# Aligned SBUF places, one sum of squares for two query tiles, and a moved filler in a two-layer trunk kernel

## The chip, the cores and the metric

The kernel runs on one core of one Trainium2 chip. The metric is the device time of one execution in microseconds (us), the median over several executions.

## The reference

A two-layer trunk step for 512 sample tokens and 128 prompt tokens, width 2048, in float32. Each layer is a pre-RMSNorm with an adaptive scale and shift (adaLN, computed from a condition vector by a 2048-row matrix), one input projection, mixers, one output projection, and a gated residual:

```python
m = jax.nn.silu(cond) @ w + b            # adaLN: shift, scale, gate
h = rms_norm(x, g) * (1 + scale) + shift
p = split_cols(h @ w_in, SPLIT)
y = concat(mixers(p)) * silu(gates)
x = x + gate * (y @ w_out)
```

The even layer mixes with banded grouped-query attention (8 heads over 2 key heads) and a gated width-3 convolution. The odd layer mixes with differential attention (two softmax maps per head, 4 heads) and with dense grouped-query attention (8 heads). Each query head of 128 columns is divided by its root mean square over the columns before it meets the keys; that is the sum of squares this change touches.

## The kernel before

The 640 tokens stand as columns, in two halves of 320 (`HV`). Every activation and every weight is held as a high and a low part, so each projection tile of 128 output columns is made of three matmuls per 128 input rows: high by high (L364), high by low (L365), low by high (L366). In later stages pairs of output tiles are made by a seven-product scheme (`run_pairs`, L667 to L669, products M1 to M7). ScalarE (ACT) rounds a weight tile to its high part (L328), VectorE (DVE) subtracts to get the low part (L329); both run a few tiles ahead of TensorE (PE), and SyncE (SP) fetches raw weights further ahead (L341). A list scheduler fixes each engine's order before the run.

The stages are: a start that loads x and computes part of adaLN on PE; the even input projection with the banded attention of four pairs of query tiles woven between its tiles (`jobs`, L1435); the rest of that projection in pairs; the even output projection; the odd input projection's gates, keys and values; the odd queries with attention (eight tiles for dense heads and eight for differential heads, in four pairs each); and the last output projection, whose tiles n = 2 to 5 are made singly (`project`, L1306) and n = 6 to 15 as five pairs p = 0 to 4.

**Query norms.** Each query tile arrives in two PSUM banks. `q_gen` (L784; `q_rider` L806 for the second dense head) copies it, squares it (ACT, L789), and calls `q_sums` (L830): three matmuls of 256 columns against a 128x32 matrix of ones (L833), at three places of the PE array, and an ACT copy of 96x256 (L836). `q_places` (L839) makes two 96x96 transposes of that copy (L842), ACT gathers six columns (L845), and GpSimd (POOL) raises 128x6 values to the power -0.5 (L851). That happens for all 24 query tiles, `q0` and `q1` of 12 pairs. The softmax of a head (`soft`, L879) takes the norms as a scale: ACT L883 and L888 use `rq`.

**The filler.** `fill2` computes one adaLN block (layer 1, block 11) on DVE beside the last output projection. It is a generator: for each of 16 row tiles POOL fetches 256 KB (L218) into one of two places, and DVE does two multiply-adds of 128x512 (`adaS<-adaw` or `adaS<-tables`, L213), then PE folds the result (L252, L259). The second place becomes a slice of `tables` at product M1 of p = 0 (`fin_rests`). Each single tile from n = 4 takes one step per quarter of its weights, so the last single tile, n = 5, which runs its token halves one after the other, takes eight. The products M6, M2, M3 and M4 of each pair take steps as well, and `begin` (L1375) drains what is left at p = 3. The block's result `hgt` is needed for output tiles 12 to 15.

**Places.** SBUF tiles are allocated in pools, one behind the other in each partition; before the change most streaming tiles start at byte 160 within a 256-byte line, while `raw`, `wh`, `wl`, `h` and `xb` start at byte 0.

The order of the weights' quarters at n = 5 is fixed in `project`:

```python
for hv in ([HV] if n < n0 - 1 else [HV[1:], HV[:1]]):
    for qd in range(4):
        proj_q(pp, parts[t + qd], qd, qd, hv)
        run_ahead(min(t + qd + 1, len(quarters) - 3))
        advance(attn, 1 if len(hv) == 2 else 2)
        if n >= fill_at:
            next(fill, None)
```

Of the kernel before, what the change touches and what calls it, by code (L numbers as in the profile page):

```python
# [20 lines left out]
P = 128  # L21
# [33 lines left out]
def trunk_kernel(ctx: ExitStack, tc: tile.TileContext, I: dict, O: dict):  # L55
# [47 lines left out]
    ident = const.tile([P, P], F32, name="ident")  # L103
    half = const.tile([P, 8], F32, name="half")
    V.memset(half[:, 0:7], -0.5)
    peps = half[:, 7:8]
    V.memset(peps, P * EPS)
# [656 lines left out]
    def k_gen(ap, pp, tag, src, gain, new_out):  # L764

        raw = ctx_keys(ap, src)
        x = stage(ap, pp)
        yield
        ss = small.tile([P, 5], F32, tag="ss", name="ss")
        kg = ap.tile([P, 5, P], F32, tag="rp", name="kg", bufs=3)  # L770
        junk = ap.tile([P, P], BF16, tag="junk", name="junk", bufs=1)
# [12 lines left out]
    def q_gen(ap, pp, tag, gain, then=None):  # L784
        x = ap.tile([P, NT], F32, tag="stg", name="qx", bufs=2)
        sq = ap.tile([P, NT], F32, tag="stg", name="qsq", bufs=2)
        for i, sl in HV:
            A.activation(x[:, sl], pp[i][:, 0:HALF], AF.Copy, scale=gain)
            A.activation(sq[:, sl], pp[i][:, 0:HALF], AF.Square)  # L789
        sw = ap.tile([P, NS], F32, tag="rp", name="qsw", bufs=st["rp"])  # L790
        for d in range(4):
            nc.sync.dma_start(sw[32 * d:32 * d + 32, :], x[32 * (d ^ 1):32 * (d ^ 1) + 32, 0:NS])
        yield
        m = ap.tile([P, NS], F32, tag="rp", name="qm", bufs=st["rp"])
        V.tensor_mul(m, x[:, 0:NS], cosT)
        sb = q_sums(ap, sq)
        yield
        V.tensor_mul(sw, sw, sinT)
        V.tensor_add(m, m, sw)
        hi, lo = q_places(ap, tag, sb)  # L800
        split(hi[:, 0:NS], lo[:, 0:NS], m)
        split(hi[:, SPLIT], lo[:, SPLIT], x[:, SPLIT])
        if then:
            attn.append(then())

    def q_rider(j, tag, gain, then=None):  # L806
        ap, (g, turned) = pools["cur"], gain
# [11 lines left out]
        sb = q_sums(ap, sq)  # L819
        yield  # L820
        V.tensor_add(m, m, sw)
        hi, lo = q_places(ap, tag, sb)
        split(hi[:, 0:NS], lo[:, 0:NS], m)
        A.activation(hi[:, SPLIT], x[:, SPLIT], AF.Copy, scale=g)
        V.scalar_tensor_tensor(out=lo[:, SPLIT], in0=x[:, SPLIT], scalar=g, in1=hi[:, SPLIT],
                               op0=ALU.mult, op1=ALU.subtract)
        if then:
            attn.append(then())

    def q_sums(ap, sq):  # L830
        ss = psT()
        for g, o in enumerate((0, 256, 384)):
            PE.matmul(ss[32 * g:32 * g + 32, 0:256], ones, sq[:, o:o + 256], start=True, stop=True,  # L833
                      tile_position=(0, 32 * g))
# [4 lines left out]
    def q_places(ap, tag, sb):  # L839
        t = psT()  # L840
        for j in range(2):
            PE.transpose(t[:, j * 96:(j + 1) * 96], sb[:, j * P:(j + 1) * P], ident[0:96, 0:96])  # L842

        u = small.tile([P, 6], F32, tag="ss", name="u")
        A.activation(u.rearrange("p (j g) -> p j g", j=2),  # L845
                     t[:, 0:192].rearrange("p (j g x) -> p j g x", j=2, g=3)[:, :, :, 0], AF.Identity, bias=peps)

        while len(attn) >= st["sets"]:
            advance(attn, 1)
        r6 = small.tile([P, 6], F32, tag="r" + tag, name="r" + tag, bufs=2)  # L850
        G.tensor_tensor(r6, u, half[:, 0:6], op=ALU.pow)  # L851
        r = [r6[:, c:c + 1] for c in (0, 3, 1, 4, 5)]
# [169 lines left out]
    nsink = const.tile([P, 8], F32, name="nsink")  # L1022
    nlam = const.tile([P, 1], F32, name="nlam")

# [5 lines left out]
    ydram = [dram.tile([P, NT], F32, name=f"yd{k}") for k in range(KT)]  # L1030
    x0dram = [dram.tile([P, 4 * NT + 1], F32, name=f"x0d{g}") for g in range(4)]
    kdram = [dram.tile([P, NT], F32, name=f"kd{k}") for k in range(10)]
# [24 lines left out]

    xTm = [sp.tile([P, 4 * NT + 1], F32, name=f"xT{g}") for g in range(4)]
    xT = [t[:, 0:4 * NT].rearrange("p (j t) -> p j t", j=4) for t in xTm]
# [61 lines left out]
    def keep(ui, n, pp):  # L1121
        g = {(6, 0): 0, (6, 4): 1, (7, 0): 2, (7, 4): 3}.get((ui, n))
        if g is not None:
            V.tensor_copy(xTm[g][:, 4 * NT:], pp[1][:, 0:1])
            nc.gpsimd.dma_start(x0dram[g], xTm[g])

# [10 lines left out]

    def q_job(tag, gain, then=None):
        return lambda pp: q_gen(pools["cur"], pp, tag, gains[gain], then)

# [67 lines left out]
    def c_job(i):  # L1208
        def f(pp):
            ap = pools["cur"]  # L1210
            z = ap.tile([P, 644], F32, tag="z", name="z", bufs=1)
            for c in (0, 513, 514, 643):
# [4 lines left out]
            V.tensor_mul(z[:, 515:643], pp[1][:, NS - HALF:HALF], u[:, SPLIT])  # L1217
            t = ap.tile([P, 642], F32, tag="rp", name="cv", bufs=3)
            V.tensor_scalar(t, z[:, 0:642], conv_w[:, 0, i:i + 1], None, ALU.mult)
# [86 lines left out]
    def project(w, cols, n0, maker, job, begin, done, tail, n_lead=3, flip=0, fill=None, rests=lambda p, name: 0.0,  # L1306
# [16 lines left out]
        for n in range(n_lead, n0):  # L1323
# [323 lines left out]
    def odd_start():  # L1647
# [5 lines left out]
        V.tensor_mul(lp, lam4[:, 0:4:2, :], lam4[:, 1:4:2, :])  # L1653
        ls = small.tile([P, 2], F32, tag="ls", name="ls", bufs=1)
        V.tensor_reduce(ls, lp, axis=AX.X, op=ALU.add)
# [14 lines left out]
    def diff_gen(ap, h, v, kq):  # L1670
# [34 lines left out]
        def weigh(u):  # L1705
# [10 lines left out]
            A.activation(on, o, AF.Copy, scale=rls[u])  # L1716
            ssq = small.tile([P, 1], F32, tag="ssq", name="ssq")
# [3 lines left out]
            rn = rns[u] = small.tile([P, 1], F32, tag="rn", name="rn")  # L1721
            G.tensor_tensor(rn, ssq, half[:, 0:1], op=ALU.pow)
            ons[u] = on
# [261 lines left out]
    def with_rest(tag, gain, rest, *a):  # L1985
        def f(pp):
            g = q_gen(pools["cur"], pp, tag, gains[gain])
# [9 lines left out]
    for h in range(4):  # L1997
        jobs.append((OD["cq"] + h * P, q_job("q0", "c_q_norm")))
        jobs.append((OD["cq"] + (4 + h) * P, with_rest("q1", "c_q_norm", head_rest, h, done0 + 4 + h)))
# [132 lines left out]
```

## Time and profile before

| what | value |
|---|---|
| median of 3 runs | 2235.76 us (2233.33 to 2236.55) |
| the profiled execution | 2232.07 us |
| its span, first to last instruction | 2230.1 us |
| busy: PE, DVE, ACT, POOL | 2198.8, 1740.5, 1139.5, 264.4 us |
| mean granted TensorE clock | 0.997 |

The profiled execution lies 3.69 us below the median of the runs, and its own time is 1.97 us longer than its span. In the rows of a timeline the first number is the start in us from the span's start and the second the duration; matmuls overlap, so the pace of PE is read from the distance between starts, not from durations. A bracket at a row's end gives the time the engine stood idle before it, and what it waited for.

### The profile page before, as it was taken

The page shows a single profiled execution, that of the slowest core. Times are in us where ns is not written, and L with a number is a line of the kernel's source. Part 1 is how long each engine was busy: PE and PEld are TensorE (multiplying, and loading weights), DVE is VectorE, ACT ScalarE, POOL GpSimd, SP SyncE. Part 2 cuts the span into 40 slices and gives each one's busy share as a digit, 9 for nine tenths or more (in the row PEclk, how much of TensorE's full clock was granted, in tenths as well). Part 3 has the DMA queues.
Part 4 walks back from the last instruction along what each step waited for, and adds up shares of the span by engine and source line. Part 5 has one row for each costly group of instructions (what it writes and reads, how often), then busy time and mean ns, then how long its engine had stood idle before and what let it go on. Part 6 is the DMA issues. An engine that isn't in the chain of part 4 may idle for free. (4 is left out here: it accounts for less than half of the span.)

```text
span 2230.1 us, 41120 instructions
## 1 busy us (share of the span) xinstructions
PE 2198.8 (99%) x15516; PEld 2126.8 (95%) x15516; DVE 1740.5 (78%) x3031; ACT 1139.5 (51%) x2445; POOL 264.4 (12%) x421
## 2 busy tenths in 40 slices
PE   7999999999999999999999999999999999999999
PEld 5899999999999999999999999999999999999999
DVE  5659898989788977877788878978667566677875
ACT  4335453535334445444654466554578766663343
POOL 3221001000000100000111112211010011111110
PEclk9999999999999999999999999999999999999999
DMA  9985556565453435844675434545532233347641
GB/s 354 342 291 180 163 167 212 175 197 167 149 160 119 145 102 171 261 127 132 218 250 155 149 92 123 177 137 160 173 98 81 73 105 110 119 139 255 200 131 52
DMA packets 380375, 368.47 MB, mean 165 GB/s; under 512 B 18946, under 2 KB 326624, under 8 KB 379664
## 3 DMA queue, kind: packets, MB, share of 16 engines
q1 hardware_dynamic: 357248, 284.78, 41.9%
q0 software_dynamic: 22064, 78.83, 10.1%
q8 instruction: 122, 2.00, 0.4%
q10 hardware_dynamic: 864, 2.23, 0.3%
q14 instruction: 77, 0.63, 0.1%
HBM read 312.41 MB, written 48.11 MB: 162 GB/s over the span
## 5 line engine op out<-in xcount | busy, mean ns | idle before, releaser
L328 ACT ACTIVATE wh<-raw 128x512 fp32r<-128x512 f32 (+1 forms) x352 | 210.6, 600 | 320.5 <-PE pb L365 206.7
L667 PE MATMUL pq<-h,wh 128*128 128x320 f32 x1152 | 359.2, 312 | 0.0
L669 PE MATMUL pq<-h,wl 128*128 128x320 f32 x1152 | 356.4, 309 | 2.7 <-DVE wl L329 2.7
L668 PE MATMUL pq<-h,wh 128*128 128x320 f32 x1152 | 356.5, 309 | 0.0
L364 PE MATMUL pa<-h,wh 128*128 128x320 f32 x944 | 300.8, 319 | 0.0
L365 PE MATMUL pa<-h,wh 128*128 128x320 f32 x944 | 295.4, 313 | 2.0 <-DVE h L329 1.9
L364 PE MATMUL pb<-h,wh 128*128 128x320 f32 x944 | 295.4, 314 | 0.0
L366 PE MATMUL pa<-h,wl 128*128 128x320 f32 x944 | 293.8, 311 | 0.0
L366 PE MATMUL pb<-h,wl 128*128 128x320 f32 x944 | 293.5, 311 | 0.1
L329 DVE TENSOR_TENSOR wl<-raw,wh 128x512 fp32r<-128x512 f32 (+1 forms) x352 | 228.5, 650 | 82.3 <-ACT wh L328 75.5
L365 PE MATMUL pb<-h,wh 128*128 128x320 f32 x944 | 292.4, 310 | 0.0
L667 PE MATMUL pq<-T,wh 128*128 128x320 f32 x864 | 268.6, 311 | 0.0
L669 PE MATMUL pq<-T,wl 128*128 128x320 f32 x864 | 267.1, 309 | 0.4 <-DVE wl L329 0.4
L668 PE MATMUL pq<-T,wh 128*128 128x320 f32 x864 | 266.9, 309 | 0.0
L328 ACT ACTIVATE wh<-sx 128x512 fp32r<-128x512 f32 x216 | 135.7, 631 | 181.3 <-PE pq L668 110.2
L669 PEld LDWEIGHTS pq<-h,wl 128*128 128x128 f32 x1152 | 216.7, 188 | 3.0 <-DVE wl L329 3.0
L667 PEld LDWEIGHTS pq<-h,wh 128*128 128x128 f32 x1152 | 216.8, 188 | 1.6 <-issue 1.6
L668 PEld LDWEIGHTS pq<-h,wh 128*128 128x128 f32 x1152 | 216.9, 188 | 0.4 <-issue 0.4
L282 DVE SCALAR_TENSOR_TENSOR acc<-adaw,sT,acc 128x1024 f32<-128x1024 f32 x150 | 189.5, 1277 | 0.0
L364 PEld LDWEIGHTS pa<-h,wh 128*128 128x128 f32 x944 | 177.9, 189 | 11.3 <-issue 10.2
L365 PEld LDWEIGHTS pa<-h,wh 128*128 128x128 f32 x944 | 178.3, 189 | 7.1 <-issue 4.5
L329 DVE TENSOR_TENSOR wl<-sx,wh 128x512 fp32r<-128x512 f32 x216 | 147.7, 688 | 43.6 <-ACT wh L328 40.7
(426 smaller groups left out, 4984.0 us busy)
## 6 DMA issues: line engine op xcount, KB each, us to landing
adaw<-in_ada_w SPq DMA_DIRECT2D x80, 512.0 KB, 4.0
raw<-in_ev_w_in SPq DMA_DIRECT2D x130, 256.0 KB, 3.3
raw<-in_od_w_in SPq DMA_DIRECT2D x112, 256.0 KB, 3.1
w<-in_od_w_in SPq DMA_DIRECT2D x48, 512.0 KB, 4.4
ada<-in_ada_w SPq DMA_DIRECT2D x11, 2048.0 KB, 13.8
adaw<-in_ada_w POOLq DMA_DIRECT2D x70, 256.0 KB, 3.4
w<-in_ev_w_in SPq DMA_DIRECT2D x27, 512.0 KB, 3.8
adah<-in_ada_w SPq DMA_DIRECT2D x20, 512.0 KB, 9.1
```

The costliest lines, as they stand in the source:

```text
L282: V.scalar_tensor_tensor(out=acc[c], in0=w, scalar=sT[:, kt, c:c + 1], in1=acc[c], op0=ALU.mult, op1=ALU.add)
L328: A.activation(hi, x, AF.Copy)
L329: V.tensor_sub(lo, x, hi)
L364: PE.matmul(ps, wh[:, i, :], hi[:, sl], start=(j == js[0] if alone else (pos == 0 and j == 0)), stop=False)
L365: PE.matmul(ps, wh[:, i, :], lo[:, sl], start=False, stop=False)
L366: PE.matmul(ps, wl[:, i, :], hi[:, sl], start=False, stop=(j == js[1] - 1 if alone else (pos == 3 and j == 3)))
L667: PE.matmul(ps, wh[:, j, :], hi, start=(first and h == 0 and j == 0), stop=False, skip_group_check=True)
L668: PE.matmul(ps, wh[:, j, :], lo, start=False, stop=False, skip_group_check=True)
L669: PE.matmul(ps, wl[:, j, :], hi, start=False, stop=(final and h == 1 and j == 3), skip_group_check=True)
```

## The change

Four edits, one diff.

1. **Places.** Small tiles are merged or padded so that the streaming tiles start at multiples of 256 bytes: `half` gets 13 columns, `nlam` moves into a spare column of `vec`, `xTm`, its DRAM copy, `junk`, `z` and `cv` are padded, `ls` and `rn` share other tiles. Work is unchanged by this, except that the copy out of `xTm` names its columns.
2. **Sums.** The squares of `q0` are kept (in a tag that has room) until `q1` comes; then one `q_sums` does four matmuls of 384 columns, one ACT copy of 128x384, three 128x128 transposes, one gather of 12 columns and one power of 128x12, and fills in both tiles' norms.
3. **Order of the jobs.** In the even stage `b2` stands before `q6`, `q7` instead of behind them.
4. **The filler.** Beside the last single tile the filler steps only with the first half of the tokens that it makes, four steps fewer; from p = 1 on, product M5 takes half a step twice.

```diff
-    half = const.tile([P, 8], F32, name="half")
-    V.memset(half[:, 0:7], -0.5)
-    peps = half[:, 7:8]
+    half = const.tile([P, 13], F32, name="half")
+    V.memset(half[:, 0:12], -0.5)
+    peps = half[:, 12:13]
...
-    def q_gen(ap, pp, tag, gain, then=None):
+    def q_gen(ap, pp, tag, gain, then=None, keep=("rp", 3)):
         x = ap.tile([P, NT], F32, tag="stg", name="qx", bufs=2)
-        sq = ap.tile([P, NT], F32, tag="stg", name="qsq", bufs=2)
+        if tag == "q0":
+            sq = st["sq0"] = ap.tile([P, NT], F32, tag=keep[0], name="qsq", bufs=keep[1])
+        else:
+            sq = ap.tile([P, NT], F32, tag="stg", name="qsq", bufs=2)
...
-        sb = q_sums(ap, sq)
+        if tag == "q1":
+            sb = q_sums(ap, st["sq0"], sq)
...
-        hi, lo = q_places(ap, tag, sb)
+        r = q_norms(sb) if tag == "q1" else []
+        hi, lo = q_places(ap, tag, r)
...
-    def q_sums(ap, sq):
+    def q_sums(ap, *sqs):
         ss = psT()
-        for g, o in enumerate((0, 256, 384)):
-            PE.matmul(ss[32 * g:32 * g + 32, 0:256], ones, sq[:, o:o + 256], start=True, stop=True,
-                      tile_position=(0, 32 * g))
-        sb = ap.tile([96, 256], F32, tag="qs", name="qs", bufs=1)
-        A.copy(sb, ss[0:96, 0:256])
+        for g in range(4):
+            PE.matmul(ss[32 * g:32 * g + 32, 0:384], ones, sqs[g // 2][:, g % 2 * 256:g % 2 * 256 + 384],
+                      start=True, stop=True, tile_position=(0, 32 * g))
+        sb = ap.tile([P, 384], F32, tag="qs", name="qs", bufs=1)
+        A.copy(sb, ss[:, 0:384])
         return sb
...
+    def q_norms(sb):
+        while len(attn) >= st["sets"]:
+            advance(attn, 1)
+        t = psT()
+        for j in range(3):
+            PE.transpose(t[:, j * P:(j + 1) * P], sb[:, j * P:(j + 1) * P], ident)
+        r = small.tile([P, 12], F32, tag="rq", name="rq", bufs=2)
+        A.activation(r.rearrange("p (j g) -> p j g", j=3),
+                     t[:, 0:384].rearrange("p (j g x) -> p j g x", j=3, g=4)[:, :, :, 0], AF.Identity, bias=peps)
+        G.tensor_tensor(r, r, half[:, 0:12], op=ALU.pow)
+        both = [[r[:, c + 2 * i:c + 2 * i + 1] for c in (0, 4, 8, 5, 9)] for i in range(2)]
+        st["q0"][2].extend(both[0])
+        return both[1]
...
-                    if n >= fill_at:
+                    if n >= fill_at and (len(hv) == 2 or hv[0][0]):
                         next(fill, None)
...
-    jobs = [u0, k0, v0, g0, q0, q1, g1, c0, b0, h0, q2, q3, u1, c1, b1, k1, v1, q4, q5, h1, u2, c2, q6, q7, b2, h2, g2, g3]
+    jobs = [u0, k0, v0, g0, q0, q1, g1, c0, b0, h0, q2, q3, u1, c1, b1, k1, v1, q4, q5, h1, u2, c2, b2, q6, q7, h2, g2, g3]
...
-        return float(name in ("M6", "M2", "M3", "M4"))
+        return {"M5": 0.5 if p else 0.0, "M6": 1.0, "M2": 1.0, "M3": 1.0, "M4": 1.0}.get(name, 0.0)
```

How the order moves is shown at two places. The first is PE at the first query pair of the even stage. Before, the sums of `q0` stand between two steps of the projection, and their transposes seven matmuls further on (`h_…` is the activation, `wh` and `wl` the weight's parts, `pa` and `pb` the banks):

```order
L366 MATMUL pa<-h_719,wl 128x320
L833 MATMUL T<-qsq,ones 32x256 x3
L364 MATMUL pa<-h_726,wh 128x320
L365 MATMUL pa<-h_726,wh 128x320
L366 MATMUL pa<-h_726,wl 128x320
L364 MATMUL pb<-h_516,wh 128x320
L365 MATMUL pb<-h_516,wh 128x320
L366 MATMUL pb<-h_516,wl 128x320
L364 MATMUL pb<-h_523,wh 128x320
L842 MATMUL T<-ident,qs 128x96 x2
```

After the change that place holds projection matmuls only, and the one insert for the pair stands where the second tile's sums stood:

```order
L365 MATMUL pb<-h_725,wh 128x320
L366 MATMUL pb<-h_725,wl 128x320
L838 MATMUL T<-qsq,ones 32x384 x4
L364 MATMUL pa<-h_907,wh 128x320
L365 MATMUL pa<-h_907,wh 128x320
L366 MATMUL pa<-h_907,wl 128x320
```

Two inserts per pair became one, of four wider matmuls.

The second place is DVE beside the last single tile of the last output projection, from the low part of that tile's third quarter to the first of the pairs' rows. Before, four filler rows (`adaS<-adaw`) stand ahead of `xr<-pa`, the row that finishes the preceding half tile:

```order
L329 TENSOR_TENSOR wl<-raw,wh 128x512
L213 SCALAR_TENSOR_TENSOR adaS<-adaw,sT,adaS 128x512
L329 TENSOR_TENSOR T_24797<-sx,T_24797 128x960
L329 TENSOR_TENSOR wl<-raw,wh 128x512
L213 SCALAR_TENSOR_TENSOR adaS<-adaw,sT,adaS 128x512
L329 TENSOR_TENSOR wl<-raw,wh 128x512
L606 TENSOR_TENSOR sx<-w_25244,raw 128x512
L213 SCALAR_TENSOR_TENSOR adaS<-adaw,sT,adaS 128x512 x2
L606 TENSOR_TENSOR sx<-w_25244,raw 128x512
L329 TENSOR_TENSOR wl<-raw,wh 128x512
L1291 SCALAR_TENSOR_TENSOR xr<-pa,hgt_137,xr 128x320
```

After the change they are gone from there, and one low part (`wl<-raw`) has moved behind the first sum `sx`:

```order
L329 TENSOR_TENSOR wl<-raw,wh 128x512
L329 TENSOR_TENSOR T_24632<-sx,T_24632 128x960
L329 TENSOR_TENSOR wl<-raw,wh 128x512
L606 TENSOR_TENSOR sx<-w_25071,raw 128x512
L329 TENSOR_TENSOR wl<-raw,wh 128x512
L606 TENSOR_TENSOR sx<-w_25071,raw 128x512
L329 TENSOR_TENSOR wl<-raw,wh 128x512
L1299 SCALAR_TENSOR_TENSOR xr<-pa,hgt_137,xr 128x320
```

Some rows further on, behind the difference `sf` of the first pair, filler rows and low parts stand in the same order in both kernels (the change has it with the same rows, its lines eight higher; the filler is two row tiles further back):

```order
L611 TENSOR_TENSOR sf<-w_25242,w_25244 128x1024
L213 SCALAR_TENSOR_TENSOR adaS<-tables,sT,adaS 128x512 x2
L213 SCALAR_TENSOR_TENSOR adaS<-adaw,sT,adaS 128x512
L1291 SCALAR_TENSOR_TENSOR xr<-pb,hgt_137,xr 128x192
L1291 SCALAR_TENSOR_TENSOR xr<-pb,hgt_137,xr 128x128
L213 SCALAR_TENSOR_TENSOR adaS<-adaw,sT,adaS 128x512
L329 TENSOR_TENSOR wl<-w_25242,wh 128x512
L213 SCALAR_TENSOR_TENSOR adaS<-tables,sT,adaS 128x512 x2
L329 TENSOR_TENSOR wl<-w_25242,wh 128x512
```

So a low part of the first pair's first product still stands behind two filler rows that read a second fetch into `tables`.

The fold of that block also moves. PE's rows L252 and L259 stood 20 matmuls apart inside p = 3; after the change L252 is issued at the end of p = 3's product M1, and L259 stands five matmuls behind it.

More of the change, by code (lines that the diff above doesn't have):

```diff
@@ L770, in k_gen @@
         kg = ap.tile([P, 5, P], F32, tag="rp", name="kg", bufs=3)
-        junk = ap.tile([P, P], BF16, tag="junk", name="junk", bufs=1)
+        junk = ap.tile([P, 160], BF16, tag="junk", name="junk", bufs=1)[:, 0:P]
         r = key_rows(x, ss, kg, junk, gain)
@@ L828, in q_rider, with q_places @@
             attn.append(then())
-    def q_sums(ap, sq):
+    def q_sums(ap, *sqs):
         ss = psT()
-        for g, o in enumerate((0, 256, 384)):
-            PE.matmul(ss[32 * g:32 * g + 32, 0:256], ones, sq[:, o:o + 256], start=True, stop=True,
-                      tile_position=(0, 32 * g))
-        sb = ap.tile([96, 256], F32, tag="qs", name="qs", bufs=1)
-        A.copy(sb, ss[0:96, 0:256])
-        return sb
[L839 to L846, printed above, removed]
+        for g in range(4):
[3 more added lines that the diff above has]
+        A.copy(sb, ss[:, 0:384])
+        return sb
+    def q_norms(sb):
         while len(attn) >= st["sets"]:
             advance(attn, 1)
-        r6 = small.tile([P, 6], F32, tag="r" + tag, name="r" + tag, bufs=2)
-        G.tensor_tensor(r6, u, half[:, 0:6], op=ALU.pow)
-        r = [r6[:, c:c + 1] for c in (0, 3, 1, 4, 5)]
+        t = psT()
[8 more added lines that the diff above has]
+        return both[1]
+    def q_places(ap, tag, r):
+        while len(attn) >= st["sets"]:
+            advance(attn, 1)
         hi, lo = (ap.tile([P, NT], F32R, tag=tag + t, name=tag + t, bufs=st["sets"]) for t in "hl")
@@ L1022, in trunk_kernel @@
     nsink = const.tile([P, 8], F32, name="nsink")
-    nlam = const.tile([P, 1], F32, name="nlam")
+    nlam = vec[:, 159:160]
     fill0 = ada_wide([(0, 8), (1, 4), (1, 0), (1, 6), (0, 10)])
@@ L1030, in trunk_kernel @@
     ydram = [dram.tile([P, NT], F32, name=f"yd{k}") for k in range(KT)]
-    x0dram = [dram.tile([P, 4 * NT + 1], F32, name=f"x0d{g}") for g in range(4)]
+    x0dram = [dram.tile([P, 4 * NT + 16], F32, name=f"x0d{g}") for g in range(4)]
     kdram = [dram.tile([P, NT], F32, name=f"kd{k}") for k in range(10)]
@@ L1054, in y_maker @@
         return make
-    xTm = [sp.tile([P, 4 * NT + 1], F32, name=f"xT{g}") for g in range(4)]
+    xTm = [sp.tile([P, 4 * NT + 64], F32, name=f"xT{g}") for g in range(4)]
     xT = [t[:, 0:4 * NT].rearrange("p (j t) -> p j t", j=4) for t in xTm]
@@ L1136, in v_job, with q_job @@
         return lambda pp: v_gen(pools["cur"], pp, src, new_out, *a)
-    def q_job(tag, gain, then=None):
-        return lambda pp: q_gen(pools["cur"], pp, tag, gains[gain], then)
+    def q_job(tag, gain, then=None, **kw):
+        return lambda pp: q_gen(pools["cur"], pp, tag, gains[gain], then, **kw)
     def y_pair(i):
@@ L1210, in f @@
             ap = pools["cur"]
-            z = ap.tile([P, 644], F32, tag="z", name="z", bufs=1)
+            z = ap.tile([P, 656], F32, tag="z", name="z", bufs=1)
             for c in (0, 513, 514, 643):
@@ L1217, in f @@
             V.tensor_mul(z[:, 515:643], pp[1][:, NS - HALF:HALF], u[:, SPLIT])
-            t = ap.tile([P, 642], F32, tag="rp", name="cv", bufs=3)
+            t = ap.tile([P, 656], F32, tag="rp", name="cv", bufs=3)[:, 0:642]
             V.tensor_scalar(t, z[:, 0:642], conv_w[:, 0, i:i + 1], None, ALU.mult)
@@ L1653, in odd_start @@
         V.tensor_mul(lp, lam4[:, 0:4:2, :], lam4[:, 1:4:2, :])
-        ls = small.tile([P, 2], F32, tag="ls", name="ls", bufs=1)
+        ls = small.tile([P, 2], F32, tag="s4", name="ls")
         V.tensor_reduce(ls, lp, axis=AX.X, op=ALU.add)
@@ L1716, in weigh @@
             A.activation(on, o, AF.Copy, scale=rls[u])
-            ssq = small.tile([P, 1], F32, tag="ssq", name="ssq")
+            both = small.tile([P, 2], F32, tag="ssq", name="ssq")
+            ssq, rns[u] = both[:, 0:1], both[:, 1:2]
             junk = ap.tile([P, 256], BF16, tag="junk", name="junk")
@@ L1720, in weigh @@
             G.tensor_scalar(ssq, ssq, 1.0 / 256, EPS, ALU.mult, ALU.add)
-            rn = rns[u] = small.tile([P, 1], F32, tag="rn", name="rn")
-            G.tensor_tensor(rn, ssq, half[:, 0:1], op=ALU.pow)
+            G.tensor_tensor(rns[u], ssq, half[:, 0:1], op=ALU.pow)
             ons[u] = on
@@ L1986, in f @@
         def f(pp):
-            g = q_gen(pools["cur"], pp, tag, gains[gain])
+            g = q_gen(pools["cur"], pp, tag, gains[gain], keep=("kk", 2))
             next(g)
@@ L1997, in trunk_kernel @@
     for h in range(4):
-        jobs.append((OD["cq"] + h * P, q_job("q0", "c_q_norm")))
+        jobs.append((OD["cq"] + h * P, q_job("q0", "c_q_norm", keep=("x2", 1))))
         jobs.append((OD["cq"] + (4 + h) * P, with_rest("q1", "c_q_norm", head_rest, h, done0 + 4 + h)))
```

8 lines of the change are left out of this document (4 added, 4 removed).

## The prediction

> **What bounds the kernel now.** I read the page's head first, then the waits of PE, then the stretches of the timeline that the change touches.
>
> ```profile
> PE 2198.8 (99%) x15516; PEld 2126.8 (95%) x15516; DVE 1740.5 (78%) x3031; ACT 1139.5 (51%) x2445; POOL 264.4 (12%) x421
> ```
>
> PE is busy for all but 1% of the span, so time is saved in two ways only: by taking instructions from PE, or by ending an idle stretch of PE. The waits of PE (line waited for, total, times, longest) show how little the second can give:
>
> ```profile
> PE T L1070 <- DMA xb<-in_x_sample: 6.6, 2, 5.0
> PE pq L669 <- DVE wl L329: 3.1, 2, 2.7
> PE T L195 <- DMA ada<-in_ada_w: 2.4, 2, 1.7
> PE T L697 <- DVE m L743: 2.0, 1, 2.0
> ```
>
> The first row is the start, where x lands. The 2.7 us of the second row lie behind the last projection's single tile, where the filler is changed.
>
> **The sums, edit 2: the main term.** PE around the insert of the first pair's second tile, its transposes for the first tile, and the filler's fold, which sends four groups where the sums send three:
>
> ```profile
> 193.51 0.31 PE L364 MATMUL pb<-h,wh 128*128 128x320 f32 x1
> 193.66 0.33 PE L842 MATMUL T<-ident,qs 96*128 96x96 f32 x2
> ...
> 194.15 0.31 PE L364 MATMUL pb<-h,wh 128*128 128x320 f32 x1
> ...
> 194.88 0.31 PE L366 MATMUL pb<-h,wl 128*128 128x320 f32 x1
> 195.12 0.63 PE L833 MATMUL T<-qsq,ones 128*32 128x256 f32 x6
> 195.68 0.42 PE L364 MATMUL pa<-h,wh 128*128 128x320 f32 x1
> 195.94 0.31 PE L365 MATMUL pa<-h,wh 128*128 128x320 f32 x1
> ```
>
> ```profile
> 484.40 0.31 PE L366 MATMUL pb<-h,wl 128*128 128x320 f32 x1
> 484.64 0.64 PE L252 MATMUL T<-acc,ones 128*32 128x256 f32 x8
> ...
> 485.46 0.30 PE L365 MATMUL pa<-h,wh 128*128 128x320 f32 x1
> ```
>
> ```profile
> 32.32 1.93 PE L195 MATMUL T<-ada,sT 128*32 128x256 f32 x32 [1.75 <-DMA ada<-in_ada_w]
> 35.16 0.64 PE L195 MATMUL T<-adah,sT 128*32 128x256 f32 x8
> ```
>
> A projection matmul follows the last after 0.147 us (194.15 to 194.88 is five of them). From the matmul ahead of the insert to the second behind it, 194.88 to 195.94, are 1.06 us; two steps of 0.147 would fill 0.29, so three groups cost 0.77 us. The fold's four groups take 484.40 to 485.46, the same 1.06: groups at different places of the array run beside each other, and a fourth is free. What more columns cost comes from the third fence: 32 records take 1.93 us and 8 take 0.64, so 24 more take 1.29, and four at a time, which is one pass of 256 columns, 0.215. Each matmul has two records (144 records for 72 matmuls), so two passes; 128 columns more are half a pass each, 0.215 in all. An insert after the change is 0.77 + 0.215 = 0.985 us, and 24 x 0.77 = 18.5 us become 12 x 0.985 = 11.8: **6.7 us less**.
>
> The bounds: if 384 columns cost no more than 256, 12 x 0.77 = 9.2 and the gain is 9.3; if the groups ran behind each other, the 0.56 us body (195.12 to 195.68) would grow by 4/3 x 384/256 to 1.12 and the insert to 1.33, 16.0 in all and a gain of 2.5. The fold's row is nearest, so I keep 6.7.
>
> Transposes: 193.51 to 194.15 are 0.64 us for three projection matmuls, which alone take 0.44, so two 96-wide ones cost 0.20. For more of them:
>
> ```profile
> 1485.17 0.31 PE L669 MATMUL pq<-T,wl 128*128 128x320 f32 x1
> 1485.32 0.71 PE L697 MATMUL T<-ident,sq 128*128 128x128 f32 x5
> ...
> 1486.01 0.31 PE L668 MATMUL pq<-T,wh 128*128 128x320 f32 x1
> ```
>
> Five cost 0.84 less 0.29, 0.55; each further one is (0.55 - 0.20) / 3 = 0.12, three cost 0.32. 24 x 0.20 = 4.8 become 12 x 0.32 = 3.8: 1.0 us less. Some inserts stand directly beside other small matmuls and share the fixed part, so of 7.7 I count **7.5 us**. All of it lies on PE, with no wait behind it.
>
> **What the later norms cost.** Norms of both tiles now come from one power of 128x12. The tightest pair is the first dense one:
>
> ```profile
> 1619.74 1.68 POOL L851 TENSOR_TENSOR rq<-u,half 128x6 f32<-128x6 f32 x1 [2.74 <-ACT u L845]
> ```
>
> ```profile
> 1623.08 0.29 ACT L883 ACTIVATE nm<-nm,rq 128x1 f32<-128x1 f32 x1 [1.24 <-DVE nm L881]
> ...
> 1624.80 0.93 ACT L983 ACTIVATE p<-p,rl 128x768 f32<-128x768 f32 x1
> ```
>
> ```profile
> 1626.58 0.38 PE L907 MATMUL T<-ident,p 128*128 128x128 f32 x2
> ```
>
> ```profile
> L851 POOL TENSOR_TENSOR rq<-u,half 128x6 f32<-128x6 f32 x24 | 38.7, 1611 | 325.4 <-ACT u L845 325.4
> L724 POOL TENSOR_TENSOR r<-ss,half 128x5 f32<-128x5 f32 x12 | 15.4, 1281 | 1.0
> ```
>
> Six columns take 1.61 us, five 1.28: in proportion twelve take 3.2 us, by the last step's 0.33 a column 3.6; that is 1.6 to 2.0 us more. The power ends at 1621.42, and ACT uses it at 1623.08, released by DVE's maximum: 1.66 us of cover. Its result p is scaled by 1625.73, and PE transposes at 1626.58: 0.85 more. 2.5 us cover 1.6 to 2.0, so I cost it at nothing. Half the ACT copies, gathers and powers fall away, on engines that are 51% and 12% busy: nothing either.
>
> **The filler, edit 4.** The rows of DVE, then of PE, around the single tile's end:
>
> ```profile
> 2072.28 0.69 DVE L606 TENSOR_TENSOR sx<-w,raw 128x512 f32<-128x512 f32 x1 [1.51 <-issue]
> 2075.55 1.54 DVE L213 SCALAR_TENSOR_TENSOR adaS<-adaw,sT,adaS 128x512 f32<-128x512 f32 x2 [2.57 <-DMA adaw<-in_ada_w]
> ...
> 2092.91 1.55 DVE L213 SCALAR_TENSOR_TENSOR adaS<-tables,sT,adaS 128x512 f32<-128x512 f32 x2 [3.38 <-DMA tables<-in_ada_w]
> ```
>
> ```profile
> 2078.85 0.93 PE L697 MATMUL T<-ident,xr 128*128 128x128 f32 x5 [1.57 <-issue]
> ...
> 2095.11 0.52 PE L669 MATMUL pq<-h,wl 128*128 128x320 f32 x1 [2.71 <-DVE wl L329]
> 2095.42 0.47 PE L667 MATMUL pq<-h,wh 128*128 128x320 f32 x1
> ```
>
> ```profile
> raw<-in_od_w_in SPq DMA_DIRECT2D x112, 256.0 KB, 3.1
> ...
> raw<-in_od_w_out SPq DMA_DIRECT2D x34, 256.0 KB, 3.9
> ```
>
> ```profile
> 2081.84 3.49 DMA tables<-in_ada_w
> ...
> 2087.20 5.62 DMA tables<-in_ada_w
> ```
>
> Two stalls of PE stand here. The first, 1.57 us, ends with `xr` behind a filler pair that waited 2.57 us for its row. The four filler rows go, so that wait goes; but the second `sx` now needs a raw weight whose fetch is issued only when a low part behind the first `sx` (2072.28) frees its place. The first `sx` takes 0.69 us and the low part about as much, so the place is free between 2073.0, when that low part starts, and 2073.6, when it ends. Such a fetch lands in 3.1 to 3.9 us, so the second `sx` starts between 2076.1 and 2077.5. Before, it starts as the filler pair ends, near 2077.0: a gain of 0.9 to a loss of 0.5. I take **0.6 us less**, since two fetches of the filler fall away from the DMA engines here.
>
> The second stall, 2.71 us, ends with a low part that stands behind filler rows waiting for the second `tables` fetch, issued at 2087.20 when the first pair of `tables` rows was read. Those rows stand in the same order after the change, and the first fetch is held by the readers of `tables` (h, L329), which do not move against PE. So this stall stays. Behind it matmuls take 0.47 us (2095.42) instead of 0.31, and the granted clock of the slice is 0.91: 9% of 20 us, 1.8 us. I keep that cost on both sides of the sum.
>
> ```profile
> 2080.00:2100.00 20.00, 17.29 (x109) 16.98 (x108) 15.44 (x27) 2.94 (x7) 4.00 (x7) 0.91 0.59 179
> ```
>
> What the trace shows is the longer matmul right behind 2.71 us of idle. [...] The measured row decides, and I keep the cost.
>
> The four filler steps come back at M5, M6 and the drain at p = 3, where DVE has room (15.44 of 20 us above). The fold's transposes now follow it by five matmuls, 0.7 us, in which ACT copies 128x256; at 20 matmuls before they did not wait. I add **0.3 us** (0 to 0.6).
>
> **The places and the job order, edits 1 and 3.** The trace has transfers into both kinds of place:
>
> ```profile
> adaw<-in_ada_w SPq DMA_DIRECT2D x80, 512.0 KB, 4.0
> ...
> w<-in_ev_w_in SPq DMA_DIRECT2D x27, 512.0 KB, 3.8
> ```
>
> The first goes to a 256-byte boundary before the change, the second 160 bytes past one; 512 KB land in 4.0 and 3.8 us. A place that mattered would show here, so I cost it at nothing, with a bound of 1 us gained, from the waits of PE for DMA other than x. [...] Moving `b2` puts the fourth pair's attention against the turn of the stage near 564 us; DVE is free for half of the slice there, so nothing waits:
>
> ```profile
> 550.00:570.00 20.00, 20.00 (x145) 18.79 (x145) 9.87 (x19) 5.43 (x12) 1.61 (x3) 1.00 0.42 134
> ```
>
> **The sum.** 2232.07 - 7.5 - 0.6 + 0.3 = 2224.3 us for an execution like the profiled one. That one lies 3.7 below the median, so the forecast on the median's scale is 2235.76 - 7.8 = **2228.0 us**, 0.35% faster.
>
> **The rivals.**
> - The second tail stall goes too. For it: the DVE chain has four rows (3.0 us) less to do, and the fetch that took 5.62 us took 3.49 the time before. Against it: the order of rows and fetches there is unchanged. It would take off 2.7 and the 1.8 of half pace: 2223.5. Chance 0.17.
> - The wide sums cost by columns and groups (the upper bound above): the gain is 2.5 + 1.0 less the tail's 0.3, 2232.6, within the noise. The fold's row speaks against it. Chance 0.18, with small losses at other waits counted in.
> - The norms come too late, the slower side. Place: each pair's first softmax. If the 12-wide power takes over 4.2 us (1.68 + 2.5 of cover), PE waits for the remainder at the first transposes of each of 12 pairs; at 5.5 us that is 12 x 1.3 = 15.6 and the time is 2243.6. For it: the power's last column cost 0.33, more than those before. Chance 0.14.
> - [...] Chance 0.06. [...]
>
> **How the numbers follow.** Forecast 0.45. A measurement of this kernel tells about 0.2%, 4.5 us, from no change: faster is under 2231.3, slower over 2240.2. Faster: 0.45 + 0.17 + 0.06, less a little for a forecast that lands at its edge, 0.65; within 0.2%: 0.21; slower 0.14. The range takes in the vanished stall and the free columns on one side (2235.76 - 9.3 - 1.0 - 4.5 = 2221) and a power a little over its cover on the other, 2239.
>
> **What would show it.** Right: the sums' insert takes about 1.28 us from the matmul ahead to the second behind; three transposes cost 0.32; PE's busy time falls by some 7 us; PE still waits 2 to 3 us for a low part near 2090 with matmuls of 0.47 us after it; the 12-wide power takes 2.9 to 3.6 us and no transposes of p wait for it. Wrong: a bracket at the first transposes of the pairs, an insert over 1.5 us, or no wait near 2090.

## The result and the profile after

| | before | after |
|---|---|---|
| median of 6 runs each | 2235.24 us (2233.33 to 2238.32) | 2226.06 us (2223.70 to 2228.38) |
| ratio | | 0.9962, 95% interval 0.9951 to 0.9973 |
| the profiled execution | 2232.07 us | 2223.70 us |
| its span | 2230.1 us | 2221.9 us |

The change makes the kernel 0.38% faster, 8.5 us by the ratio and 9.2 us between the medians. Both profiled executions are faster than their kernel's median, by 3.2 and 2.4 us. The forecast was 7.8 us faster (2228.0 us, range 2221 to 2239). The head of the page of the changed kernel, to be read against the one in the prediction:

```profile
span 2221.9 us, 40941 instructions
...
PE 2191.2 (99%) x15456; PEld 2121.7 (95%) x15456; DVE 1738.2 (78%) x3031; ACT 1134.9 (51%) x2421; POOL 256.2 (12%) x409
```

PE's busy time fell by 7.6 us and the span by 8.2; PE still works for 99% of it. The insert for a pair's sums, in the timeline of PE, stands like this now:

```profile
192.46 0.31 PE L366 MATMUL pb<-h,wl 128*128 128x320 f32 x1
192.70 0.85 PE L838 MATMUL T<-qsq,ones 128*32 128x384 f32 x8
193.48 0.41 PE L364 MATMUL pa<-h,wh 128*128 128x320 f32 x1
193.73 0.30 PE L365 MATMUL pa<-h,wh 128*128 128x320 f32 x1
```

From the matmul ahead to the second behind are 1.27 us, 0.98 more than two steps of 0.147; the prediction had 0.985. The three transposes, at the second pair, where projection matmuls stand on both sides:

```profile
276.24 0.31 PE L366 MATMUL pb<-h,wl 128*128 128x320 f32 x1
276.39 0.49 PE L849 MATMUL T<-ident,qs 128*128 128x128 f32 x3
...
276.86 0.31 PE L365 MATMUL pa<-h,wh 128*128 128x320 f32 x1
```

They take 0.62 less 0.29, 0.33 us; the prediction had 0.32. Added up over all inserts in the same way, the sums fell from 19.0 to 12.5 us and the transposes from 5.1 to 3.8: 7.8 us less in all.

The groups of GpSimd's powers (instructions, busy us, mean ns) give the price of the wider one:

```profile
L853 POOL TENSOR_TENSOR rq<-rq,half 128x12 f32<-128x12 f32 x12 | 30.4, 2536 | 301.4 <-ACT rq L851 301.4
```

Twelve columns take 2.54 us, below the 2.9 to 3.6 that were expected.

Matched by the projections' matmuls, the two profiled executions drift apart in four places: 1.6 us before PE's first projection matmul, 2.0 us over the even stage's four pairs, 3.7 us over the odd stage's eight pairs with 1.7 given back at their end, and 3.5 us at the last projection's single tile. The rest comes and goes within 1.6 us. The waits behind the last two, in PE's timeline of the changed kernel:

```profile
1999.28 0.44 PE L1739 MATMUL T<-ident,on 128*128 128x128 f32 x2 [1.83 <-DVE on L1734]
```

```profile
2073.90 0.93 PE L697 MATMUL T<-ident,xr 128*128 128x128 f32 x5 [1.45 <-ACT h L328]
2089.88 0.77 PE L697 MATMUL T<-ident,xr 128*128 128x128 f32 x5 [0.66 <-DVE xr L1299]
```

The first row belongs to the attention's last step: PE comes earlier and waits for DVE. The second row is the first tail stall, nearly as long as before (1.45 against 1.57 us). The second tail stall, 2.71 us before, has no row of its own any more: the largest idle time there is 0.66 us, and the matmuls behind it take 0.31 us as usual. At the start and at the tail this execution is the quickest of all 14 profiles in this document, so its 1.6 and 3.5 us there are not what the change brings in the mean.

### The profile page after: what moved, and what is told of

It reads as the page before. It is cut to its first block, busy times and chain, and to the rows that moved or that the text cites. A ratio compares the mean times of both kernels' runs of the same rounds, so it can differ in the third digit from the quotient of the medians.

```text
span 2221.9 us, 40941 instructions
## 1 busy us (share of the span) xinstructions
PE 2191.2 (99%) x15456; PEld 2121.7 (95%) x15456; DVE 1738.2 (78%) x3031; ACT 1134.9 (51%) x2421; POOL 256.2 (12%) x409
## 4 chain that ended last, share of the span: by engine, by line
PE 90%; DVE 3%; DMA 3%; issue 2%; ACT 2%; POOL 1%; SPq 0%; ACTq 0%; DVEq 0%; POOLq 0%
PE pq L667 13%; PE pq L669 13%; PE pq L668 13%; PE pa L364 6%; PE pa L365 6%; PE pa L366 6%; PE pb L364 6%; PE pb L366 5%; PE pb L365 5%; PE T L915 2%; PE S L927 1%; PE T L195 1%; PE S L928 1%; PE S L929 1%; PE T L697 1%
## 6 DMA issues: line engine op xcount, KB each, us to landing
ada<-in_ada_w SPq DMA_DIRECT2D x11, 2048.0 KB, 12.5
```

## The experiments

Each run was timed beside the kernel before on the same chip; "ratio" is against that. Differences from the changed kernel are differences of two ratios, each good to about 0.1%, so 3 us is what they can tell. The kernels with one edit alone or one edit undone split the gain; the others test prices and waits.

### The places alone, and the change without them

`places` is the kernel before with edit 1; `off` is the changed kernel with its places shifted back by one spare tile:

```diff
+    small.tile([P, 40], F32, tag="pad", name="pad", bufs=1)
```

> The kernel before with edit 1 alone (the places at multiples of 256 bytes; same work in the same order). Theory P (the prediction's: places cost nothing): within 2 us of the kernel before, the start's 2048 KB loads still land in about 13.8 us, and the second stall beside the last projection still ends near 2.7 us of idle. Theory T (places shorten transfers): 2 to 6 us faster; the 2048 KB loads land in about 12.5 us as in the changed kernel, PE reaches its first projection matmul 1.6 us earlier, and the two 512 KB loads that collide with the second fetch into tables take nearer 4.7 than 6.7 us together, so that the second stall is gone.

> The changed kernel with one spare tile of 160 bytes put ahead of the stages, so that all its streaming tiles lie 160 bytes past a multiple of 256 again; nothing else differs. Theory P: the same time as the changed kernel, 9 us below the kernel before. Theory T: 2 to 6 us of that are lost again, so 3 to 7 us below before; the start's loads land in 13.8 us again and the second stall is back.

Measured: `places` 2232.35 us, ratio 0.9990 (0.9980 to 0.9999); `off` 2228.77 us, ratio 0.9971 (0.9959 to 0.9982), where the changed kernel has 0.9962. Both say about 2 us for the places, at the lower end of theory T, but the interval of the first runs from 0.2 to 4.5 us, and the second, 2.0 us, is good only to 3.6. The 2048 KB loads of the start (KB each, median us to landing), in `off`, in the changed kernel and in `places`:

```profile
ada<-in_ada_w SPq DMA_DIRECT2D x11, 2048.0 KB, 13.8
```

```profile
ada<-in_ada_w SPq DMA_DIRECT2D x11, 2048.0 KB, 12.5
```

```profile
ada<-in_ada_w SPq DMA_DIRECT2D x11, 2048.0 KB, 12.8
```

Over all 14 profiles they land in 13.1 to 13.8 us at the old places (five profiles) and in 12.5 to 12.8 at a multiple of 256 bytes (nine), 7% earlier in the mean. The first projection matmul of PE starts at 36.84 us in `off`, at 35.12 in the changed kernel:

```profile
36.84 0.56 PE L365 MATMUL pa<-h,wh 128*128 128x320 f32 x2
```

```profile
35.12 0.56 PE L364 MATMUL pa<-h,wh 128*128 128x320 f32 x2 [0.22 <-ACT h L1121]
```

These two profiles lie far apart. Over all 14 it starts between 36.71 and 37.52 us at the old places and between 35.12 and 36.30 at the new ones, with one at 37.33; the means differ by 1.1 us. Away from the start, loads of 512 KB show nothing of the kind: in `off` and in the changed kernel the weights `w<-in_od_w_in` land in 4.1 us and `w<-in_ev_w_in` in 3.7 (the first profile of before, with the old places as in `off`, has 4.4 and 3.8). Loads of 128 KB that run beside the large ones (`raw`, issued by POOL) land in 5.1 us where those are at a multiple of 256 bytes and in 5.4 to 5.5 where they are not.

### The start's places alone

`start_off` shifts the start's pool only:

```diff
+    pre.tile([P, 40], F32, name="spare")
     rows_a, rows_b, th = (pre.tile([P, P], F32, name=n) for n in ("rows_a", "rows_b", "th"))
```

> The changed kernel with a spare tile of 160 bytes at the head of the start's pool alone: the start's 2048 KB loads lie 160 bytes past a multiple of 256 again, every later stage keeps its place, and every engine's order is the same. Theory S (the places pay at the start only): the loads land in 13.8 us instead of 12.5, PE's first projection matmul comes 0.8 to 1.6 us later, and the whole loss of the run with all places shifted (about 2 us) is seen. Rival (the places pay in every stage): at most a third of it, 0.3 to 0.7 us.

Measured: 2226.24 us, ratio 0.9966 (0.9953 to 0.9979), 0.9 us by the ratios; the loads are back at 13.7 us, and PE's first projection matmul starts at 37.52 us:

```profile
ada<-in_ada_w SPq DMA_DIRECT2D x11, 2048.0 KB, 13.7
```

```profile
PE T L196 <- DMA ada<-in_ada_w: 3.6, 2, 3.0
```

PE waits 3.6 us for them, against 0.2 in the changed kernel. But that wait does not belong to the places: `nojobs` (below) has the new places, its loads land in 12.8 us, and PE waits 4.2 us for them and starts its first projection matmul at 37.33:

```profile
PE T L195 <- DMA ada<-in_ada_w: 4.2, 2, 3.1
```

In both profiles the transposes of x were through some 1.7 us earlier than in the changed kernel, and PE had the time to wait. So what is shown is that the loads land earlier, and a start that is about 1 us earlier in the mean of the profiles. That this is what the times gain is likely, not shown: the 0.9 us of `start_off` lies inside its interval, and neither theory S nor its rival can be ruled out.

### The sums

`nosums` is the kernel before with edits 1, 3 and 4; `sums_twice` issues each joint sum's matmuls twice:

```diff
-        for g in range(4):
+        for g in (0, 1, 2, 3, 0, 1, 2, 3):
```

> The kernel before with edits 1, 3 and 4, without the joint sums of edit 2. Theory P (the joint sums carry 5.7 to 7.5 us): 2 to 4 us faster than before. Rival (the joint sums are given back at other waits, the gain is places and filler): 6 to 9 us faster than before, like the changed kernel.

> The changed kernel with each joint sum's four matmuls issued twice (the second set writes the same values). By the insert's measured 0.78 us body, two passes of 384 columns at 0.323 us are added to each of 12 inserts: 0.65 us each, 7.8 us in all, if PE's time passes through to the end. If PE's time is partly taken back by waits behind it (theory of the give-back), 4 to 6 us slower than the changed kernel.

Measured: `nosums` 2232.18 us, ratio 0.9987 (0.9978 to 0.9996), so the joint sums are worth 0.25%, 5.6 us. `sums_twice` 2234.84 us, ratio 1.0008 (0.9999 to 1.0017), 0.46% or 10.3 us slower than the changed kernel. The page of `nosums`:

```profile
PE 2199.0 (99%) x15516; PEld 2125.1 (95%) x15516; DVE 1740.5 (78%) x3031; ACT 1138.0 (51%) x2445; POOL 264.8 (12%) x421
```

PE's busy time differs by 7.8 us from the changed kernel's, as much as the inserts release. In `sums_twice` the insert is longer by what was expected, 1.92 us instead of 1.27 from neighbour to neighbour, 0.65 more:

```profile
192.82 0.31 PE L366 MATMUL pb<-h,wl 128*128 128x320 f32 x1
193.06 1.50 PE L838 MATMUL T<-qsq,ones 128*32 128x384 f32 x16
...
194.74 0.31 PE L365 MATMUL pa<-h,wh 128*128 128x320 f32 x1
```

The 10.3 us that this costs have an interval of some 3, so they agree with 7.8 put on and passed through. The 5.6 us of `nosums` have one as wide and can't tell 7.8 from 4.6.

The traces can. Each profile is cut at the same projection matmuls, at 36.7, 607.5, 1569.3 and 2054.6 us of the kernel before; the stretches with query pairs are the first and the last. The five profiles without joint sums (`before`, `before_again`, `places`, `filler`, `nosums`) are compared in the mean with six that have them (the changed kernel, `off`, `start_off`, `nofill`, `early_norms`, `nojobs`); both groups hold old and new places and both fillers. The first stretch, with four pairs, is 2.5 us shorter (good to 1.6), and 7.8 / 12 = 0.65 a pair make 2.6. The last, with eight pairs, is 2.1 us shorter (485.0 against 482.9, good to 0.6), where 5.2 were released. So about 4.6 of 7.8 us arrive, which agrees with 5.6 by the times. The rival, a gain that is given back, is right for some 3 us, all in the odd stage. PE's idle time there rises from 4.2 to 5.4 us, the wait for `on` shown above among it; where the rest is lost is open.

### The filler

`filler` is the kernel before with edit 4; `nofill` is the changed kernel with edit 4 undone:

```diff
-                    if n >= fill_at and (len(hv) == 2 or hv[0][0]):
+                    if n >= fill_at:
...
-        return {"M5": 0.5 if p else 0.0, "M6": 1.0, "M2": 1.0, "M3": 1.0, "M4": 1.0}.get(name, 0.0)
+        return float(name in ("M6", "M2", "M3", "M4"))
```

> The kernel before with edit 4 alone (the filler's four steps moved). Theory P: 0 to 2 us faster, with the second stall still there. Rival (the four missing filler rows end the second stall, with the low clock behind it): 3.5 us faster, idle ahead of the low part under 1 us as in the changed kernel.

> The changed kernel with edit 4 undone: the four filler rows stand beside the last single tile again. If the missing rows are what shortened the second stall behind that tile, it is back with 2.7 us of idle and the kernel is 2 to 4 us slower than the changed one. If edit 4 is worth 0 to 1 us (as its run alone suggests: ratio 0.9997) and the stall follows how the loads happen to land, it is within 1 us of the changed kernel, 8 us below before.

Measured: `filler` 2233.50 us, ratio 0.9997 (0.9988 to 1.0006); `nofill` 2225.18 us, ratio 0.9964 (0.9950 to 0.9978). Edit 4 is worth nothing that these runs can see, from either side. To see whether the second stall belongs to the filler's order, the kernel before was profiled again:

> The kernel before, profiled once more. If the second stall behind the last single tile belongs to the kernel, it ends at 2.7 us of idle again with a low clock after it; if it follows how the loads happen to land, it has another size, between 0 and 3 us, at the same place in the order.

Its one run took 2235.94 us. The rows on which the stall depends, the second pair of filler rows that read `tables`, in DVE's timeline: in `before_again`, with the old filler and the old places; in `nofill`, with the old filler and the new places; in `filler`, the other way about; and in the changed kernel:

```profile
2096.79 1.55 DVE L213 SCALAR_TENSOR_TENSOR adaS<-tables,sT,adaS 128x512 f32<-128x512 f32 x2 [2.70 <-DMA tables<-in_ada_w]
```

```profile
2085.77 1.55 DVE L213 SCALAR_TENSOR_TENSOR adaS<-tables,sT,adaS 128x512 f32<-128x512 f32 x2 [1.66 <-DMA tables<-in_ada_w]
```

```profile
2091.70 1.55 DVE L213 SCALAR_TENSOR_TENSOR adaS<-tables,sT,adaS 128x512 f32<-128x512 f32 x2 [2.59 <-DMA tables<-in_ada_w]
```

```profile
2085.30 1.55 DVE L213 SCALAR_TENSOR_TENSOR adaS<-tables,sT,adaS 128x512 f32<-128x512 f32 x2 [1.05 <-DMA tables<-in_ada_w]
```

The wait for that fetch is there in every kernel, with either filler, 1.05 to 3.38 us long. The stall of PE behind it mostly follows: 2.71 and 2.31 us in the two profiles of before, 1.43 in `filler`, 1.29 in `places`, 0.80 in `nofill`, under 0.7 in the changed kernel. It is missing in `nosums` and `sums_twice`, though DVE waits 2.60 and 2.12 us there: in these two the matmuls behind the first tail stall take 0.47 us for a while (in `nosums` from 2082.79 to 2085.45), and PE comes late enough not to wait again. The first stall is no steadier, 1.57 and 2.62 us in the two profiles of before, 2.29 in `nofill`, 1.78 in `filler`, 2.69 in `nosums`. So the four filler rows alone did not decide it. In the changed kernel the two 512 KB loads in flight beside this fetch landed 4.8 and 5.2 us after their issue, in the first profile of before 7.8 and 7.9; both profiles of before have old places and the longest stalls. `off` has old places as well and waits only 1.63 us, though, in its row:

```profile
2088.13 1.55 DVE L214 SCALAR_TENSOR_TENSOR adaS<-tables,sT,adaS 128x512 f32<-128x512 f32 x2 [1.63 <-DMA tables<-in_ada_w]
```

What sets the landing is not settled.

### The norms, late and early

The prediction's slower side was a power that comes too late. `late_norms` and `half_late` put two or one powers of 128x6, unused, ahead of each power; `early_norms` splits it so that q0's columns come first:

```diff
+        for i in (0, 6):
+            G.tensor_tensor(small.tile([P, 6], F32, tag="ss", name="spare"), r[:, i:i + 6], half[:, 0:6], op=ALU.pow)
         G.tensor_tensor(r, r, half[:, 0:12], op=ALU.pow)
```

```diff
-        G.tensor_tensor(r, r, half[:, 0:12], op=ALU.pow)
+        for i in (0, 2):
+            r3 = r.rearrange("p (j g) -> p j g", j=3)[:, :, i:i + 2]
+            G.tensor_tensor(r3, r3, half[:, 0:12].rearrange("p (j g) -> p j g", j=3)[:, :, i:i + 2], op=ALU.pow)
```

> The changed kernel with two powers of 128x6 on GpSimd ahead of each power of 128x12, their results unused: the norms of each pair come about 3.2 us later and PE's order is the same. By the cover of 2.5 us, worked out ahead of the run at the tightest pair for a power of 1.68 us (so 4.2 us from the gather to the norms), 5.7 us is 1.5 us over at that pair: 1 to 12 us slower than the changed kernel, with brackets at the first transposes of p. Rival (the cover is wider than worked out, the softmax runs behind by a whole turn): no difference.

> The changed kernel with one power of 128x6 ahead of each power of 128x12, its result unused: the norms come about 1.6 us later, half of the run with two (which was 27 us slower than the changed kernel). Theory E (the cover at the even stage's pairs is some 0.5 us, as the first pair's rows of the changed kernel show: norms ready at 200.87, used by DVE at 201.02, the matmul that needs what follows starts 0.33 us after its operand): 8 to 14 us slower than the changed kernel, with PE's brackets at the scores of q1. Theory C (the cover of 2.5 us in the prediction; 1.6 us of delay on 2.5 us of power make 4.1): no difference.

> The changed kernel with the power of 128x12 made in two of 128x6, q0's columns first: q0's norms come about 1 us earlier, q1's some 0.7 us later, the order of PE is the same. If the part of the joint sums' gain that is missing (7.5 expected, 5.6 measured) is lost to norms that come late, 1 to 2 us faster than the changed kernel. If no wait for norms is left in the changed kernel, the same within 1 us.

Measured: `late_norms` 2252.29 us, ratio 1.0084 (1.0069 to 1.0099), 27 us slower than the changed kernel, far over what was expected. `half_late` 2233.13 us, ratio 0.9991 (0.9982 to 1.0000), 6.5 us slower. `early_norms` 2228.24 us, ratio 0.9966 (0.9953 to 0.9978), the same within the intervals. The first pair of the even stage shows why. The changed kernel's POOL, DVE, ACT and PE:

```profile
198.03 2.84 POOL L853 TENSOR_TENSOR rq<-rq,half 128x12 f32<-128x12 f32 x1 [17.05 <-ACT rq L851]
```

```profile
201.02 0.27 DVE L893 TENSOR_SCALAR nm<-nm,rq,nsink 128x1 f32<-128x1 f32 x1
```

```profile
202.15 0.62 ACT L328 ACTIVATE q1h<-qm 128x512 fp32r<-128x512 f32 x1
```

```profile
203.10 0.28 PE L927 MATMUL S<-k0h,q1h 128*128 128x256 f32 x1
```

The power ends at 200.87 and DVE uses it at 201.02. The row behind that one on DVE, `qm<-qm,qsw` (L803), does not read the norms and starts at 201.20; ACT makes the softmax and then `q1h`, which ends at 202.77, and PE multiplies by it at 203.10. The cover is 0.15 us on DVE and 0.33 on PE. With one more power in `half_late`, DVE waits and PE waits:

```profile
203.37 0.27 DVE L894 TENSOR_SCALAR nm<-nm,rq,nsink 128x1 f32<-128x1 f32 x1 [2.16 <-POOL rq L854]
```

```profile
203.06 0.31 PE L366 MATMUL pa<-h,wl 128*128 128x320 f32 x1
205.16 0.38 PE L928 MATMUL S<-k0h,q1h 128*128 128x256 f32 x1 [1.79 <-ACT q1h L328]
```

DVE's use comes 2.35 us later, of which this profile runs 0.10 late anyway, and `qm<-qm,qsw` comes behind it again, at 203.56, 2.36 us later. PE would have gone on 0.15 us behind 203.06 and loses 1.95: between DVE's use and PE there is 0.3 us of cover, as the 0.33 above says, and some 0.5 with DVE's 0.15. Theory C, the cover of 2.5 us, falls; theory E stands, with a smaller sum than it gave because not every pair is as tight: PE's brackets at the scores of q1 are 1.79, 1.11 and 1.74 us at the first, third and fourth pair of the even stage, and the second has none. The times of `early_norms` can't tell 1 to 2 us from nothing, but its odd stage is as long as the changed kernel's, 483.4 and 483.3 us by the cuts above, so late norms are not what takes the missing 3 us there. The changed kernel stands just ahead of that edge.

### The order of the jobs

`nojobs` is the changed kernel with edit 3 undone:

```diff
-    jobs = [u0, k0, v0, g0, q0, q1, g1, c0, b0, h0, q2, q3, u1, c1, b1, k1, v1, q4, q5, h1, u2, c2, b2, q6, q7, h2, g2, g3]
+    jobs = [u0, k0, v0, g0, q0, q1, g1, c0, b0, h0, q2, q3, u1, c1, b1, k1, v1, q4, q5, h1, u2, c2, q6, q7, b2, h2, g2, g3]
```

> The changed kernel with edit 3 undone (b2 behind q6 and q7 again). Prediction: edit 3 costs and brings nothing, within 1 us of the changed kernel. Rival: the fourth pair, whose attention ends at the turn, pays or gains 2 us or more around 500 to 564 us.

Measured: 2225.61 us, ratio 0.9954 (0.9941 to 0.9966), against 0.9962 (0.9951 to 0.9973) for the changed kernel: no difference that can be told. By the intervals the edit could bring 2 us or cost 5. No kernel tried is shown to beat the changed one.

## Why the prediction was right

- **The joint sums: the price right, the way to the end not.** The insert's price held to 0.01 us (0.98 against 0.985), and the transposes' (0.33 against 0.32). That a fourth group is free (1.06 us with three and with four) and that 128 more columns cost half a pass more (0.215 us for 256), read from the fold and from the start's loop, held: two passes of 384 added 0.65 us to the insert in `sums_twice`. 7.5 us were counted as taken from PE, and 7.8 were taken. What failed is "with no wait behind it": in the odd stage 2.1 of 5.2 us arrive, some 4.6 of 7.8 in all by the traces, 5.6 by the times with an interval of some 3.
- **The norms at no cost: right in the result, wrong in the reason.** The step that failed is "the tightest pair is the first dense one". The even stage's first pair is tighter: some 0.5 us of cover by `half_late`, not 2.5. That it went well was luck: at that pair the power took 2.84 us, which with 0.5 of cover makes 3.3, and the prediction's range for the power ran from 3.2 to 3.6. The slower rival was the right mechanism with too high a threshold: 4.2 us was named, and a delay of one more power already costs 6.5 us.
- **The places at nothing: the reason wrong, the size open.** "A place that mattered would show here" was argued from 512 KB loads; those don't show it. The start's loads of 2048 KB do: 13.8 us became 12.5. The places bring about 2 us by the times, good to some 2, and about 1 us at the start by the profiles, so the bound of 1 us is not clearly broken. The 0.06 in the sum of the chances, for shorter transfers that shorten the wait at L743 too, is a term that no run shows: that wait is 1.9 to 2.1 us in all 14 profiles, loads of 512 KB take 4.1 and 3.7 us in `off` and in the changed kernel alike, and only the start's large loads came earlier by 1.3 us, with some 0.3 for the small ones beside them.
- **The filler: the direction of one stall wrong, the sum right.** The first stall was to shrink by 0.6 us and shrank by 0.1; the second was to stay and fell under 0.7 in the profiled execution, one of the three signs that the prediction named for being wrong. Yet edit 4 by itself gives nothing in the times of either pair of runs. What the prediction missed is that the second stall's length differs from one kernel's profile to the next; the price of 2.7 + 1.8 us was read from one execution.
- **The job order at nothing: not contradicted**, within the wide interval of `nojobs`.
- **A slip in a rival.** With the tail's 0.6 less and 0.3 more, the rival on the wide sums comes to 2232.0 us, not 2232.6.

By the runs' medians the sum is then 5.6 for the sums, about 2 for the places, 0 to 1 for the filler and 0 for the order: 7.6 to 8.6, against 8.5 by the ratio. Each term is good to 2 or 3 us. As far as these terms can be trusted, the forecast of 7.8 came close partly by luck, since a first term counted too high and a second one counted too low offset each other.

## What to carry to other kernels

Price an instruction on a full engine by the distance between its neighbours' starts, with and without it, and the width that isn't in the trace by a loop that repeats the same form; that gave the insert's price to 1%. But time taken from a full engine is not yet time gained: cut several profiles at the same instructions and see how much of it arrives. Before calling a delay covered, look at every place where it recurs, and follow what stands behind the waiting instruction in its engine's order: in `half_late` the next row of DVE, which needed no norm, came 2.36 us later too. A stall that hangs on a landing transfer is worth what several profiles say it is (the second tail stall from under 0.7 to 2.71 us), and transfers of one size can say little about others: in `off` and in the changed kernel 512 KB landed in 4.1 us, 2048 KB in 13.8 and 12.5.

## What the runs showed of the hardware

**Places count for the large loads of the start.** 2048 KB loads land in 13.1 to 13.8 us at 160 bytes past a multiple of 256, in 12.5 to 12.8 at a multiple. Loads of 512 KB away from the start show no difference: 4.1 and 3.7 us at either place in `off` and the changed kernel. Why the large ones land earlier is not shown.

**The same idle time is not always followed by the low clock.** PE idles 1.9 to 2.1 us ahead of the key's transposes in all 14 profiles (L743), and in ten of them the matmuls behind are longer for a while, in four of these ten only from 0.8 to 1.2 us after the restart on. Behind it matmuls take 0.47 us for about 3 us in the changed kernel, where the granted clock was 0.50 from 173 to 176 us; in `filler` they take 0.31 at once:

```profile
172.43 0.70 PE L697 MATMUL T<-ident,m 128*128 128x128 f32 x4 [1.98 <-DVE m L743]
...
173.20 0.47 PE L365 MATMUL pa<-h,wh 128*128 128x320 f32 x1
```

```profile
174.84 0.66 PE L697 MATMUL T<-ident,m 128*128 128x128 f32 x4 [1.98 <-DVE m L743]
...
175.48 0.31 PE L365 MATMUL pa<-h,wh 128*128 128x320 f32 x1
```

Behind the 2.71 us of the second tail stall in the first profile of before, the granted clock was 0.50 from 2096 to 2098 us. The prediction kept 1.8 us for that as if it belonged to the stall; behind the waits at L743 the slower matmuls came in ten profiles of 14, not in all.
